# Moving row squares between VectorE and ScalarE in an RMS-norm and GELU kernel

## Chip, cores, metric

The kernel runs on one core of one Trainium2 chip. The metric is the device time of an execution in microseconds (us); medians of several executions are given. The span of a profiled execution is about 2 us shorter than the time on the metric.

## The reference

```python
x: (8, 1024, 2048) float32, gamma: (2048,), eps = 1e-5
rms = np.sqrt(np.mean(x ** 2, axis=-1, keepdims=True) + eps)
out = gamma * x / rms
return 0.5 * out * (1 + np.tanh(np.sqrt(2 / np.pi) * (out + 0.044715 * out ** 3)))
```

67.1 MB come in and 67.1 MB go out, in float32.

## The kernel before

The 8192 rows are cut into 16 groups of 128 partitions by 4 rows (4096 KB each). Six groups fit in SBUF at a time, in six slots. For each group SyncE issues the load. ScalarE and VectorE square the four rows and sum each (ScalarE with an activation and accumulator, VectorE with a product of the row with itself). VectorE and GpSimd make 1/rms. VectorE multiplies the group by gamma, in place. ScalarE applies GELU with 1/rms as its scale, in place, and issues the store. A slot's next load waits until its store has landed. Groups 2 and 3 come in with one double load, and groups 12 and 13 go out with one double store. "Landing" is the moment at which the program learns that a transfer is complete.

```python
def on_vector(g):
    return 1 if g % 3 else 2        # how many of the 4 squares VectorE does

def squares(g, r, n):               # on ScalarE
    for q in range(r, r + n):
        nc.scalar.activation(out=junk, in_=slot[g % SLOTS][:, q, :],
                             func=ACT.Square, accum_out=ssq[:, g, q : q + 1])

def squares_on_vector(g, r, n):
    for q in range(r, r + n):
        row = slot[g % SLOTS][:, q, :].rearrange("p (a b) -> p a b", b=GW)
        nc.vector.scalar_tensor_tensor(out=spare[:, :, 0:GW], in0=row, scalar=1.0, in1=row,
            op0=ALU.bypass, op1=ALU.mult, accum_out=ssq[:, g, q : q + 1])

# ... (inverse_rms, scale, gelu, store as described above)

for g in range(G + 1):              # each engine runs its own share of this in this order
    if g < G:
        squares(g, 0, R - on_vector(g))
        squares_on_vector(g, R - on_vector(g), on_vector(g))
        # ... inverse_rms(g); scale(g, 0, R)
    if g:
        gelu(g - 1)
        store(g - 1)
        if g - 1 + SLOTS < G:
            load(g - 1 + SLOTS)
```

Note the order on ScalarE: the squares of group g stand ahead of the GELUs of group g - 1, and so ahead of the store of group g - 1.

Of the kernel before, what the change touches and what calls it, by code (L numbers as in the profile page):

```python
# [13 lines left out]
SLOTS = 6  # L14
# [10 lines left out]
def kernel(  # L25
# [51 lines left out]

    def on_vector(g):

        return 1 if g % 3 else 2  # L80

    def load(g):
        nc.sync.dma_start(out=slot[g % SLOTS], in_=part(x2, g))  # L83
# [70 lines left out]
    with tc.manual_schedule():  # L154
# [23 lines left out]
        for g in range(G + 1):  # L178
# [3 lines that stand above are left out]
                if g < G - 1:  # L182
                    inverse_rms(g)
                    scale(g, 0, R)
                else:
                    scale(g, 0, 1)
                    inverse_rms(g)
                    for r in range(1, R):
                        scale(g, r, 1)
# [5 lines that stand above are left out]
# [35 lines left out]
```

## Time and profile before

| | before |
|---|---|
| time, median | 317.19 us (6 runs, 316.85 to 317.45) |
| span of the profiled run | 315.1 us |
| VectorE busy | 198.5 us, 63% |
| ScalarE busy | 206.9 us, 66% |
| load queue and store queue | 49.7% and 49.3% of 16 DMA engines |
| squares on ScalarE / VectorE | 42 / 22 |

The busy shares of the compute engines are averages over stages.

### The profile page before, as it was taken

How to read it: one execution, taken by the hardware profiler on the slowest of the kernel's cores; microseconds unless marked ns; L12 is line 12 of the kernel's file. 1: busy time of each engine (PE TensorE's matmuls, PEld its weight loads, DVE VectorE, ACT ScalarE, POOL GpSimd, SP SyncE). 2: the span in 40 equal slices, each digit the busy share in tenths (PEclk: the TensorE clock that was granted, in tenths of full speed). 3: DMA queues.
4: the chain of work that ended last, by engine and by line, in shares of the span. 5: the costliest groups of instructions: out<-in, count | busy, mean ns of one | idle time of the engine just before them, and what ended most of it. 6: DMA issues, size and time to landing. Idle time of an engine off the chain costs nothing.

```text
span 315.1 us, 457 instructions
## 1 busy us (share of the span) xinstructions
PE 7.2 (2%) x8; PEld 2.5 (1%) x8; DVE 198.5 (63%) x129; ACT 206.9 (66%) x150; POOL 16.4 (5%) x21
## 2 busy tenths in 40 slices
PE   0900000000000000000000000000000000000000
PEld 0300000000000000000000000000000000000000
DVE  0089887988989884639684393668727638781000
ACT  1327869999999749397590965929369295797000
POOL 0010101011010101010010100101001010010000
DMA  8999989999999999999999999999999999999896
GB/s 334 404 462 408 526 339 396 458 402 462 403 463 403 459 408 458 412 453 424 441 424 441 424 441 424 441 428 437 437 428 437 428 437 428 474 399 474 387 445 291
DMA packets 4498, 134.24 MB, mean 426 GB/s; under 512 B 512, under 2 KB 656, under 8 KB 656
## 3 DMA queue, kind: packets, MB, share of 16 engines
q1 hardware_dynamic: 2160, 67.11, 49.7%
q10 hardware_dynamic: 2336, 67.12, 49.3%
q14 instruction: 2, 0.02, 0.0%
HBM read 67.12 MB, written 67.11 MB: 426 GB/s over the span
## 4 chain that ended last, share of the span: by engine, by line
another core or an unknown queue 36%; DMA 36%; ACT 18%; issue 1%; SPq 1%; ACTq 0%
DMA pair<-in_x_dram 21%; DMA out_dram<-pair 15%; ACT pair L133 12%; ACT junk L87 6%; SPq L83 1%; ACTq L143 0%
## 5 line engine op out<-in xcount | busy, mean ns | idle before, releaser
L124 DVE TENSOR_TENSOR pair<-pair,gamma_ps 128x8192 f32<-128x8192 f32 (+1 forms) x19 | 139.2, 7334 | 0.0
L87 ACT ACTIVATE junk<-pair 128x2048 f32<-128x2048 f32 x42 | 79.0, 1881 | 78.7 <-DMA pair<-in_x_dram 76.2
L133 ACT ACTIVATE pair<-pair,rstd 128x2048 f32<-128x2048 f32 x64 | 122.6, 1987 | 2.3 <-DVE pair L124 1.9
L97 DVE SCALAR_TENSOR_TENSOR spare<-pair 128x2048 f32<-128x2048 f32 x22 | 50.4, 2291 | 39.3 <-DMA pair<-in_x_dram 24.6
L110 POOL TENSOR_TENSOR y<-ms,power 128x4 f32<-128x4 f32 x16 | 16.1, 1007 | 260.8 <-DVE ms L105 260.8
L105 DVE TENSOR_SCALAR ms<-ssq 128x4 f32<-128x4 f32 x16 | 2.7, 170 | 26.2 <-ACT junk L87 25.4
L113 DVE TENSOR_TENSOR z<-ms,y 128x4 f32<-128x4 f32 x16 | 2.6, 163 | 19.0 <-POOL y L110 19.0
L87 ACT ACTIVATION_READ_ACCUMULATOR junk<-pair 128x1 f32 x42 | 7.8, 186 | 0.0
L171 PE MATMUL gamma_ps<-spare,ones 1*128 1x512 f32 x8 | 7.2, 1072 | 8.3 <-DMA spare<-in_gamma_dram 8.3
L117 DVE SCALAR_TENSOR_TENSOR rstd<-z,y 128x4 f32<-128x4 f32 x16 | 2.6, 162 | 0.6
L114 DVE SCALAR_TENSOR_TENSOR z<-z,y 128x4 f32<-128x4 f32 x16 | 2.6, 162 | 0.6
L171 PEld LDWEIGHTS gamma_ps<-spare,ones 1*128 1x128 f32 x8 | 2.5, 326 | 11.4 <-issue 11.4
L169 ACT ACT_TABLE_LOAD x1 | 1.3, 1283 | 1.4 <-PEq L211 1.4
L97 DVE DVE_READ_ACCUMULATOR spare<-pair 128x1 f32 x22 | 1.8, 83 | 0.0
L167 DVE MEMSET warm<- 1x1 f32 x1 | 0.1, 59 | 0.8 <-PEq L211 0.8
L169 ACT ACTIVATE warm<-warm 1x1 f32<-1x1 f32 x1 | 0.2, 202 | 0.0
L168 DVE MEMSET ones<- 1x128 f32 x1 | 0.2, 165 | 0.0
L166 POOL MEMSET power<- 128x4 f32 x1 | 0.1, 101 | 0.3 <-POOLq L211 0.3
L211 POOL MEMSET const-float32-0.0<- 128x1 f32 x1 | 0.1, 98 | 0.2 <-issue 0.2
L211 POOL MEMSET const-bfloat16-1.0<- 128x1 bf16 x1 | 0.1, 102 | 0.0
L211 POOL MEMSET const-uint8-127<- 128x1 uint8 x1 | 0.1, 102 | 0.0
L211 POOL MEMSET const-float32-1.0<- 128x1 f32 x1 | 0.1, 98 | 0.0
## 6 DMA issues: line engine op xcount, KB each, us to landing
pair<-in_x_dram SPq DMA_DIRECT2D x14, 4096.0 KB, 25.5
out_dram<-pair ACTq DMA_DIRECT2D x13, 4096.0 KB, 52.4
out_dram<-pair ACTq DMA_DIRECT2D x1, 4032.0 KB, 31.3
out_dram<-pair ACTq DMA_DIRECT2D x1, 64.0 KB, 17.6
spare<-in_gamma_dram ACTq DMA_DIRECT2D x1, 8.0 KB, 7.4
pair<-in_x_dram SPq DMA_DIRECT2D x1, 40.5
out_dram<-pair ACTq DMA_DIRECT2D x1, 30.9
```

Of the source, the lines that this page charges most:

```text
L83: nc.sync.dma_start(out=slot[g % SLOTS], in_=part(x2, g))
L87: nc.scalar.activation(out=junk, in_=slot[g % SLOTS][:, q, :], func=ACT.Square, accum_out=ssq[:, g, q : q + 1],)
L97: nc.vector.scalar_tensor_tensor(out=spare[:, :, 0:GW], in0=row, scalar=1.0, in1=row, op0=ALU.bypass, op1=ALU.mult, accum_out=ssq[:, g, q ...
L105: v.tensor_scalar(out=ms, in0=ssq[:, g, :], scalar1=1.0 / D, scalar2=eps_f, op0=ALU.mult, op1=ALU.add,)
L110: nc.gpsimd.tensor_tensor(out=y_, in0=m_, in1=power, op=ALU.pow)
L113: v.tensor_tensor(out=z_, in0=m_, in1=y_, op=ALU.mult)
L114: v.scalar_tensor_tensor(out=z_, in0=z_, scalar=-0.5, in1=y_, op0=ALU.mult, op1=ALU.mult)
L117: v.scalar_tensor_tensor(out=rstd[:, g, :], in0=z_, scalar=1.5, in1=y_, op0=ALU.add, op1=ALU.mult,)
L124: nc.vector.tensor_tensor(out=rows, in0=rows, in1=gamma_ps.unsqueeze(1).to_broadcast([P, n, D]), op=ALU.mult,)
L133: nc.scalar.activation(out=slot[g % SLOTS][:, r, :], in_=slot[g % SLOTS][:, r, :], func=ACT.Gelu_apprx_tanh, scale=rstd[:, g, r : r + 1],)
L169: nc.scalar.activation(out=warm, in_=warm, func=ACT.Gelu_apprx_tanh)
L171: nc.tensor.matmul(out=gamma_ps[:, k : k + 512], lhsT=ones, rhs=gamma_row[:, k // GW : (k + 512) // GW, 0:GW], start=True, stop=True,)
```

## The change

The intent is to relieve ScalarE while the slots fill for the first time, when it is busy nearly all the time, and to give VectorE less to do later on.

```diff
     def on_vector(g):
 
-        return 1 if g % 3 else 2
+        return 2 if g < SLOTS else 1
```

SLOTS is 6. The counts do not change: 22 squares on VectorE and 42 on ScalarE in both kernels.

## The prediction

> **What bounds the kernel now.** I read the page first: the strip of DMA load over the span, then the shares of the two queues. VectorE is busy for 63% of the span, ScalarE for 66%; neither is near full. The transfers are.
>
> ```profile
> DMA  8999989999999999999999999999999999999896
> DMA packets 4498, 134.24 MB, mean 426 GB/s; under 512 B 512, under 2 KB 656, under 8 KB 656
> q1 hardware_dynamic: 2160, 67.11, 49.7%
> q10 hardware_dynamic: 2336, 67.12, 49.3%
> ```
>
> q1 carries the loads of x, q10 the stores of the result. Together their packets fill 49.7 + 49.3 = 99.0% of the time of 16 engines: of 315.1 us only about 3 us are not transfer. To see where those 3 us lie, I asked for the busy table in six stretches that follow the kernel's stages: start, loads alone, the mixed stage while the slots fill and drain for the first time, the steady state, stores alone, end.
>
> ```profile
> 0.00:5.00 5.00, 0.00 (x0) 0.00 (x0) 0.22 (x2) 1.49 (x2) 0.31 (x5) 1.00 0.68 236
> 5.00:45.00 40.00, 7.16 (x8) 2.49 (x8) 26.77 (x17) 20.50 (x17) 2.02 (x2) 1.00 1.00 432
> 45.00:110.00 65.00, 0.00 (x0) 0.00 (x0) 55.75 (x39) 61.09 (x44) 5.03 (x5) 1.00 1.01 432
> 110.00:270.00 160.00, 0.00 (x0) 0.00 (x0) 102.14 (x62) 104.96 (x77) 8.05 (x8) 1.00 1.00 433
> 270.00:310.00 40.00, 0.00 (x0) 0.00 (x0) 13.61 (x12) 18.90 (x12) 1.01 (x1) 1.00 1.00 433
> 310.00:315.00 5.00, 0.00 (x0) 0.00 (x0) 0.00 (x0) 0.00 (x0) 0.00 (x0) 1.00 0.52 223
> ```
>
> The last two columns are DMA share and GB/s; before them stand length, then busy us of PE, weight load, VectorE, ScalarE and GpSimd, and the clock. From 5 to 310 us the engines are full at 432 to 433 GB/s, whether they load, store or do both. The only gaps are the first 2 us before any packet moves and the run-out after the last. So 134.24 MB / 0.4325 = 310.4 us, plus about 2 us of start, 0.7 us of run-out and 1 to 2 us around them, is the 315.1 us span. A change that moves no bytes has nothing to win here; it can only lose, by leaving a queue empty.
>
> Note the stretch 45 to 110: ScalarE is busy 61.09 of 65 us there, and VectorE 55.75. This is the stage that the change is aimed at, and the one that looks compute-bound if the DMA column is overlooked.
>
> The second question is how far the stores are issued ahead of need. The page's list of DMA issues, with KB each and median us from issue to landing:
>
> ```profile
> pair<-in_x_dram SPq DMA_DIRECT2D x14, 4096.0 KB, 25.5
> out_dram<-pair ACTq DMA_DIRECT2D x13, 4096.0 KB, 52.4
> ```
>
> A group is 4096 KB = 4.19 MB; alone it needs 4.19 / 0.432 = 9.7 us, and with both queues alternating 19.4 us. A store takes 52.4 us, so the typical one stands in its queue for about 52.4 - 19.4 = 33 us before a byte of it moves. The chain of waits shows the same for one store:
>
> ```profile
> 81.91 45.95 DMA out_dram<-pair
> ```
>
> Store 3 was issued at 81.91 and landed at 127.86.
>
> **What the Trainium skill says.** "Perfetto Trace Analysis", section "Roofline", says that one core alone is bounded by its 16 DMA engines at about 435 GB/s in total; the 432 to 433 GB/s above agree, and say that there is no headroom. "DMA: Bandwidth & Descriptors", section "Queues, rings and completion order", says that each DMA engine takes turns between the queue rows for which it has work. The trace agrees: from 45 to 110 us q1 moved 14.61 MB and q10 13.42 MB. A queue with anything in it therefore gets its half, and the engines idle only if both are empty. "ScalarE: Activation LUTs", section "What ACT_TABLE_LOAD costs", gives an activation with immediate operands as 186 ns + 0.833 ns per element, 1892 ns for 2048; the Square activations here took 1881 ns, so the price of a moved square is the ordinary one.
>
> **The change part by part.** Counts first. Before, groups 0, 3, 6, 9, 12 and 15 have two squares on VectorE: 16 + 6 = 22. After, groups 0 to 5 have two: 12 + 10 = 22. ScalarE keeps 42. Nothing is added or removed: groups 1, 2, 4, 5 hand one square each to VectorE, groups 6, 9, 12, 15 take one each back. Busy times stay near 198.5 and 206.9 us.
>
> Steps as the timeline has them, start to start. On VectorE: a group with one square takes 12.83 us (73.84 to 86.67), with two 15.15 us (58.69 to 73.84); the 8.68 us scaling of the group is the last part. On ScalarE: a square 2.03 us, four Gelus 7.66, store issue to next square 0.4.
>
> Early stage. VectorE starts group 1 at 30.64 as before. With 15.15 us each, groups 2 to 6 start at 45.8, 60.9, 76.1, 91.2, 106.4 (before: 43.5, 58.7, 73.8, 86.7, 99.5), and each group's scaling ends as the next starts. ScalarE now has only 2 squares and finishes them early, then waits for the scaling:
> - store 1: squares of group 2 from 42.16, done 46.2; Gelus to 53.9 (before 55.83, so 1.9 us earlier);
> - store 2: scaling done 61.0, plus 7.7: 68.7 (before 67.86);
> - store 3: 76.2 + 7.7 = 83.9 (before 81.91);
> - store 4: 91.3 + 7.7 = 99.0 (before 95.97);
> - store 5: 106.5 + 7.7 = 114.2 (before 108.00, so 6.2 us later).
>
> So the change moves the early bound from ScalarE to VectorE and makes stores 2 to 5 later by 0.8, 2.0, 3.0 and 6.2 us. What does this cost? Store 0 is untouched and lands at 69.8, where load 6 is issued. From there a store lands every 19.4 us, so store 1 has its turn at about 69.8, store 2 at 89, store 3 at 108.5 (landing 127.86, as measured), store 4 at 128, store 5 at 147. Issued at 53.9, 68.7, 83.9, 99.0 and 114.2 they are 16, 20, 25, 29 and 33 us early. Cost: 0.
>
> Group 6 has one square: VectorE starts group 7 at 106.4 + 12.8 = 119.2. Its load landed at 114.79; ScalarE does its three squares from then to 120.9, and store 6 goes out at 128.5, just as before. From there loads set the rhythm again and the delay is forgotten.
>
> Steady state. In groups 9 and 12 ScalarE does three squares, so stores 8 and 11 go out 2.03 us later (165.15 to 167.2, 223.22 to 225.2). ScalarE then waits 7.74 us for the next load in those periods and would wait 5.7 us, as in its other groups. Cost: 0.
>
> Tail. This is the only place where a later store could show at the end.
>
> ```profile
> 269.65 1.88 ACT L87 ACTIVATE junk<-pair 128x2048 f32<-128x2048 f32 x1 [5.67 <-DMA pair<-in_x_dram]
> ...
> 281.29 0.34 ACTq L143 DMA_DIRECT2D out_dram<-pair  x1
> 281.67 7.68 ACT L133 ACTIVATE pair<-pair,rstd 128x2048 f32<-128x2048 f32 x4 [0.42 <-ACT pair L133]
> 289.38 0.34 ACTq L143 DMA_DIRECT2D out_dram<-pair  x1
> ```
>
> The last load lands at 269.65; group 15 now has three squares on ScalarE, so store 14 goes out at 281.29 + 2.03 = 283.3 and store 15 at 291.4. VectorE keeps up: its inverse waits for the third square at 275.7, and the last scaled row is ready at about 284.3, well before the last Gelu asks for it near 289.5. The double store of groups 12 and 13 was issued at 264.01 and took 30.9 us (its own line of the issue list), so it lands at 294.9. Store 14 moves from then, store 15 from 294.9 + 9.7 = 304.6. Both are still 11.6 and 13.2 us early. Cost: 0.
>
> Sum: 0.0 us. I predict 317.2 us, the time before.
>
> **The rivals.** First, VectorE becomes the bound in the early stage. It does: from 15 to 119 us it is nearly always busy. If this stage were on the path, the late store 5 would add up to 6.2 us, for 323.4 us (2.0% slower). Against it: the 20 us and more by which these stores lead the queue, and that q10 isn't empty.
>
> Second, the intent works: if the 61.09 of 65 us of ScalarE were the bound of the early stage, four squares taken off would give 4 x 2.03 = 8.1 us, 309 us (2.6% faster). Against it: the 1.01 DMA share of the same stretch, and that 310.4 us of bytes alone forbid it.
>
> Third, the tail shows its 2.03 us in full: 319.2 us. It would if the queue ran dry before 291.4; for that over 11 us of backlog would have to be gone.
>
> Fourth, the other mix of early loads and stores changes the DMA rate itself. The rate is 432 or 433 in all stages, so I would give this 0.5 us at most, either way.
>
> **Range and chances.** The three runs before spread over 0.6 us. The central case is exactly 0, each margin is over 10 us, and what is left is noise and the third rival in part: 316.6 to 318.0 us. Faster by over 2% (below 310.9) is ruled out by the bytes: 0.01. Slower by over 2% (above 323.6) needs an error in the backlog: 0.02. Within 2%: 0.97.
>
> **What would show each step.** Right: q1 and q10 again 49 to 50% each and DMA share 1.00 in the stretches between 5 and 310 us; load 6 issued near 69.8 us; store 5 issued near 114, stores 14 and 15 near 283.3 and 291.4; median landing of the stores shorter by their later issue, with the same landing times; ScalarE waiting for the scaling between 60 and 107 us. Wrong: a stretch after 45 us with a DMA share below 0.97, loads from the seventh on issued later than before, or an end of the span after 316 us.

## More of the kernel before

The waits say who sits idle for whom. Two lines of the waits of the kernel before (who waited, for whom, us in total, times, longest us):

```profile
ACT junk L87 <- DMA pair<-in_x_dram: 76.2, 12, 10.1
ACT pair L133 <- DVE pair L124: 1.9, 1, 1.9
```

L87 is the Square on ScalarE, L133 the GELU, L124 the scaling by gamma on VectorE. ScalarE waits for loads for 76 us in all, and for VectorE's scaling only once.

## The result and the profile after

| | before | after |
|---|---|---|
| time, median | 317.19 us (6 runs, 316.85 to 317.45) | 317.22 us (6 runs, 316.98 to 317.27) |
| span of the profiled run | 315.1 us | 315.3 us |
| VectorE busy | 198.5 us | 198.5 us |
| ScalarE busy | 206.9 us | 207.4 us |

The ratio is 1.0, with a 95% interval of 0.9987 to 1.0013. Ratios here are the mean time of one kernel's fast runs over that of the other's fast runs of the same rounds, so they are not quite the ratio of the medians quoted.

The page of the changed kernel, load strip and queues:

```profile
DMA  8999989999999999999999999999999999999896
q1 hardware_dynamic: 2160, 67.11, 49.8%
q10 hardware_dynamic: 2336, 67.12, 49.3%
```

The strip is the same digit for digit. The busy table of the changed kernel in the six stretches of the prediction (last two columns: DMA share and GB/s; of the numbers with a count (x), the third and fourth are VectorE and ScalarE busy us):

```profile
0.00:5.00 5.00, 0.00 (x0) 0.00 (x0) 0.22 (x2) 1.49 (x2) 0.31 (x5) 1.00 0.71 242
5.00:45.00 40.00, 7.16 (x8) 2.49 (x8) 26.61 (x18) 18.46 (x15) 2.02 (x2) 1.00 1.00 432
45.00:110.00 65.00, 0.00 (x0) 0.00 (x0) 58.44 (x40) 53.20 (x38) 4.76 (x5) 1.00 1.01 430
110.00:270.00 160.00, 0.00 (x0) 0.00 (x0) 101.61 (x61) 113.11 (x84) 8.34 (x9) 1.00 1.00 433
270.00:310.00 40.00, 0.00 (x0) 0.00 (x0) 11.60 (x10) 21.11 (x14) 1.01 (x1) 1.00 1.00 433
310.00:315.00 5.00, 0.00 (x0) 0.00 (x0) 0.00 (x0) 0.00 (x0) 0.00 (x0) 1.00 0.58 249
```

The DMA columns of this view count a packet (mostly 32 KB, 1.2 us here) whole in the stretch in which it begins: a short stretch can read above 1.00, and 0.00 means that no packet begins.

From 45 to 110 us ScalarE went from 61.09 to 53.20 us and VectorE from 55.75 to 58.44. The work moved, as intended; the DMA columns hardly did (share 1.01 in both, 432 and 430 GB/s). The waits of the changed kernel, the same two lines:

```profile
ACT junk L87 <- DMA pair<-in_x_dram: 66.0, 12, 10.3
ACT pair L133 <- DVE pair L124: 13.9, 5, 3.9
```

ScalarE now waits five times for VectorE's scaling, 13.9 us in all. It waits 10 us less for loads. This is one idle time in exchange for another. The timeline shows it at one place of the early stage, and the stores at the tail:

```profile
61.21 7.68 ACT L133 ACTIVATE pair<-pair,rstd 128x2048 f32<-128x2048 f32 x4 [2.94 <-DVE pair L124]
...
114.39 0.34 ACTq L143 DMA_DIRECT2D out_dram<-pair  x1
...
283.52 0.34 ACTq L143 DMA_DIRECT2D out_dram<-pair  x1
...
291.62 0.34 ACTq L143 DMA_DIRECT2D out_dram<-pair  x1
```

The GELUs of group 2 start 2.94 us after ScalarE is free, when the scaling is done. Store 5 is issued at 114.39, 6.4 us later than before, and stores 14 and 15 at 283.52 and 291.62, 2.2 us later. The median time of a store from issue to landing fell accordingly:

```profile
out_dram<-pair ACTq DMA_DIRECT2D x13, 4096.0 KB, 50.4
```

It was 52.4. Stores that are issued later stand in the queue for less, and land when they landed before: every store of the changed kernel landed within 0.5 us of its landing before (store 3 at 128.20 in place of 127.86).

### The profile page after: what moved, and what is told of

Its sections match the earlier page's. It is cut to its first block, busy times and chain, and to the rows that moved or that the text cites. A ratio compares the mean times of both kernels' runs of the same rounds, so it can differ in the third digit from the quotient of the medians.

```text
span 315.3 us, 455 instructions
## 1 busy us (share of the span) xinstructions
PE 7.2 (2%) x8; PEld 2.5 (1%) x8; DVE 198.5 (63%) x129; ACT 207.4 (66%) x150; POOL 16.4 (5%) x21
## 3 DMA queue, kind: packets, MB, share of 16 engines
q1 hardware_dynamic: 2160, 67.11, 49.8%
q10 hardware_dynamic: 2336, 67.12, 49.3%
## 4 chain that ended last, share of the span: by engine, by line
DMA 42%; DVE 22%; ACT 17%; another core or an unknown queue 6%; PE 2%; issue 2%; POOL 2%; SPq 0%; ACTq 0%; DVEq 0%; POOLq 0%
DMA pair<-in_x_dram 24%; DMA out_dram<-pair 15%; DVE pair L124 14%; ACT pair L133 11%; DVE spare L97 7%; ACT junk L87 5%; DMA spare<-in_gamma_dram 2%; PE gamma_ps L171 2%; POOL y L110 2%; DVE ms L105 0%; DVE z L113 0%; DVE z L114 0%; DVE rstd L117 0%; SPq L83 0%
## 5 line engine op out<-in xcount | busy, mean ns | idle before, releaser
L133 ACT ACTIVATE pair<-pair,rstd 128x2048 f32<-128x2048 f32 x64 | 122.7, 1988 | 14.3 <-DVE pair L124 13.9
## 6 DMA issues: line engine op xcount, KB each, us to landing
pair<-in_x_dram SPq DMA_DIRECT2D x14, 4096.0 KB, 25.4
```

The costliest lines, as they stand in the source:

```text
L133: nc.scalar.activation(out=slot[g % SLOTS][:, r, :], in_=slot[g % SLOTS][:, r, :], func=ACT.Gelu_apprx_tanh, scale=rstd[:, g, r : r + 1],)
```

## The experiments

The median of the kernel before in the same rounds was 317.02, 316.97 or 317.0 us. The theory: the DMA engines are full, and each store is issued long before the store queue reaches it, so that moved squares cost or gain nothing. The rivals: the early and the late half of the change cancel; VectorE or the tail is on the path; moving squares between these engines costs nothing anywhere.

### The halves of the change alone

```diff
# early half alone
-        return 1 if g % 3 else 2
+        return 2 if g < SLOTS or g % 3 == 0 else 1
# late half alone
-        return 1 if g % 3 else 2
+        return 2 if g < SLOTS and g % 3 == 0 else 1
```

> The early half of the change alone: two squares on VectorE in groups 0 to 5, two in every third group after that, as before. Theory (full DMA engines, both halves cost nothing): 317.2 us, within 0.3. Rival (the halves cancel: the early half gains or loses by itself what the late half gives back): off 317.2 by 2 us or more, in the opposite sense to the late half. If the later store 5 (114.3 in place of 108.0) were on the path: 323. Stores 14 and 15 are issued near 281.5 and 289.6 as before the change.

Measured: 317.15 us (5 runs), ratio to before 1.0002 (0.999 to 1.0015).

> The late half alone: groups 0 to 5 as before, one square on VectorE in every group from 6 on. Theory: 317.2 us, within 0.3; stores 14 and 15 issued 2.0 us later, near 283.5 and 291.6, with the same end. Rival (the tail shows its square): 319.2. Rival (halves cancel): off by 2 us or more, opposite to the early half.

Measured: 317.24 us (5 runs), ratio 1.0007 (0.9995 to 1.002). Stores 14 and 15 were issued at 283.27 and 291.36.

Neither half moves the median by more than some 0.2 us (the wider interval leaves room for 0.6), so no gain and loss of 2 us or more cancel. Each is hidden by itself.

### How large the margins are: the tail

The changed kernel, with row 0 of group 15 squared n more times on ScalarE ahead of the last GELUs (n = 4, then 8; the result stays right):

```diff
                 squares(g, 0, R - on_vector(g))
+                if g == G - 1:
+                    for _ in range(n):
+                        squares(g, 0, 1)
```

> The changed kernel with row 0 of group 15 squared four more times on ScalarE (8.1 us, result unchanged) ahead of the last Gelus. Stores 14 and 15 go out near 291.6 and 299.7. By the margins (the store queue reaches them at 294.9 and 304.6 in the kernel before) both are still in time: 317.2 us, within 0.4. Rival (the tail is on the path): 325.3 us. If a store needs some 3 us or more between issue and first packet even at the head of the queue, up to 1 us shows.

Measured: 317.24 us (4 runs), ratio 1.0008 (0.999 to 1.0026). 8.1 us of extra work on ScalarE directly ahead of the last two stores cost nothing.

> The same with eight more squares (16.3 us). Store 14 goes out near 299.8, 5 us after the queue is empty at about 295; store 15 near 307.9, before store 14 has moved. Theory: 5 us of empty engines and about 2 us from issue to first packet, so 322 to 325 us, with a DMA share well below 1.00 between 295 and 302 us. Rival (tail on the path from the start): 333 us. Rival (the margin is larger than counted): 317.

Measured: 323.67 us (4 runs, 323.45 to 323.79), ratio 1.0207 (1.0192 to 1.0223). The busy table from 295 to 302 us, first with four extra squares:

```profile
295.00:302.00 7.00, 0.00 (x0) 0.00 (x0) 0.00 (x0) 4.66 (x3) 0.00 (x0) 1.00 1.01 435
```

and with eight, together with the two 3 us stretches after 293 us:

```profile
295.00:302.00 7.00, 0.00 (x0) 0.00 (x0) 6.18 (x6) 6.58 (x4) 0.72 (x1) 1.00 0.35 150
...
293.00:296.00 3.00, 0.00 (x0) 0.00 (x0) 1.78 (x4) 3.00 (x3) 1.01 (x1) 1.00 0.00 0
296.00:299.00 3.00, 0.00 (x0) 0.00 (x0) 2.96 (x4) 3.00 (x2) 0.00 (x0) 1.00 0.00 0
```

With four, the engines are full (1.01). With eight, store 14 goes out at 299.77, the queue has run dry, and from 293 to 300 us no packet begins. The packet records of this trace (start and duration of each) tell more exactly when nothing moves: the engines finish the double store between 293.8 and 294.8 us, close to the 295 expected, and the first packet of store 14 begins at 300.61, 0.84 us after its issue, where the expectation had about 2. The time lost against the changed kernel is 323.67 - 317.22 = 6.45 us, and the engine time that stands idle in these records between 290 and 303 us is 6.6 us for all 16 engines, so the dry queue accounts for the whole loss. Both kernels behave as the margins say, and the two together bracket the margin: 8.1 us are free and 16.3 us cost 6.45, so the margin is about 16.3 - 6.45 = 9.8 us on top of the 2.2 us that the change itself used. That is 12 us for store 14 of the kernel before, where the prediction had 11.6 + 2.0 = 13.6. The 0.84 us from issue to first packet, which the prediction left out, is a good half of the difference (the Trainium skill, "DMA: Bandwidth & Descriptors", section "Latency and other measured facts", gives about 0.6 us to the first byte, a little less than this trace shows); the ragged end of the double store, up to 1 us, can account for most of the rest.

### How large the margins are: the early stage

The changed kernel with three squares of each of the first six groups on VectorE, with four, and with four and the last row squared a second time:

```diff
-        return 2 if g < SLOTS else 1
+        return 3 if g < SLOTS else 1        # three;  4 for the runs with four
...
                 squares_on_vector(g, R - on_vector(g), on_vector(g))
+                if g < SLOTS:                       # only in the run "four and one again"
+                    squares_on_vector(g, R - 1, 1)
```

Three:

> Three of the four squares of groups 0 to 5 on VectorE, 17.5 us a group. Estimate: stores 1 to 5 issued near 58, 76, 93, 111 and 128, so 11 to 19 us ahead of their turns at 70, 89, 108.5, 128 and 147. Theory: 317.2 us within 0.4, and a spread as small as that of the kernel before. The load of group 5 waits here for gamma's transfer, as in the run with four squares (the build gives it a shared semaphore); if that wait is what made those runs scatter from 317.4 to 319.8, these scatter too.

Measured: 317.04 us (5 runs, 316.87 to 317.51), ratio 1.0001 (0.9989 to 1.0013). Stores 1 to 5 were issued at 58.39, 75.89, 93.38, 110.87 and 128.36, as estimated. Store 5 is 20 us later than in the kernel before, and the time is the same. The extra wait of one load did no harm.

Four, twice:

> All four squares of groups 0 to 5 on VectorE: 19.8 us for each of these groups. Estimate from the durations of the traces: store 0 issued at 43 (38.6 in the changed kernel), stores 1 to 5 at about 63, 83, 103, 122 and 142, against turns in the store queue at 70, 89, 108.5, 128 and 147. So each is still about 5 us ahead, and the theory says 317.2 us, within 0.6. Rival (VectorE sets the early stage, any delay shows): store 5 is 28 us later than in the changed kernel, so up to 345 us; a rival in which lateness costs in part as it grows: 319 or more.

Measured: 317.39, 317.79 and 319.80 us, and one run of 324.93; ratio 1.0041 (1.0011 to 1.0071).

> The run with all four early squares on VectorE again, with more rounds: its fast executions read 317.39, 317.79 and 319.80 us, one slower 324.93. If the 5 us of margin are about used up, the same scatter comes back (317 to 320, now and then more), and the run with three squares lacks it. If the scatter was that chip's, all five agree within 0.6 us of 317.5.

Measured: 318.35 to 320.5 us in five runs, and one run of 324.8 labelled slow; ratio 1.0084 (1.0064 to 1.0104). The label rests on the time alone (over 1.5% above the fastest; the granted clock is 1.0 as in the others), and no other kernel here has such a run, so these two may belong to the scatter; the ratios leave them out. The scatter came back on another occasion and the kernel with three squares lacks it, so it belongs to this kernel. My expectation that a margin of some 5 us is as good as a larger one was wrong by 0.4 to 0.8%.

The engines did not run out of work here before the end: in the profiled run of 320.0 us the DMA share was 1.00 or 1.01 in every stretch from 5 to 310 us. But the load queue did run empty once. The two queues from 72 to 76.5 us (packets, MB, share of 16 engines), first in this run, then in the changed kernel:

```profile
q10 hardware_dynamic: 67, 2.10, 110.7%
q1 hardware_dynamic: 15, 0.00, 0.2%
...
q10 hardware_dynamic: 33, 1.08, 55.6%
q1 hardware_dynamic: 46, 0.98, 50.7%
```

The expectation noted that store 0 would be issued later, but gave it no margin to overdraw. Its landing starts load 6, the first load that has to wait for a slot. In this run store 0 was issued at 43.17 in place of 38.59, landed at 72.89 in place of 70.06, and so load 6 went out 2.8 us later, when the first loads had all moved. The store queue filled the engines meanwhile, so none stood idle, but the loads stayed late: the last one landed at 273.87 in place of 269.83. In the other profiled run with four squares (317.79 us) the last load landed at 271.36. With three squares store 0 still landed at 69.47 and the last load at 268.49.

What differs in time is the run-out. The busy table of that run after 310 us:

```profile
310.00:312.00 2.00, 0.00 (x0) 0.00 (x0) 0.00 (x0) 0.00 (x0) 0.00 (x0) 1.00 0.95 410
312.00:314.00 2.00, 0.00 (x0) 0.00 (x0) 0.00 (x0) 0.00 (x0) 0.00 (x0) 1.00 0.46 197
314.00:316.00 2.00, 0.00 (x0) 0.00 (x0) 0.00 (x0) 0.00 (x0) 0.00 (x0) 1.00 0.19 82
```

and of the changed kernel:

```profile
310.00:312.00 2.00, 0.00 (x0) 0.00 (x0) 0.00 (x0) 0.00 (x0) 0.00 (x0) 1.00 1.06 459
312.00:314.00 2.00, 0.00 (x0) 0.00 (x0) 0.00 (x0) 0.00 (x0) 0.00 (x0) 1.00 0.38 164
```

After 310 us there are 2 x (410 + 197 + 82) = 1378 KB left against 2 x (459 + 164) = 1246, only 132 KB more, which is 0.3 us for all 16 engines. But from 314 to 316 us the share is 19%, as much as some three of the sixteen engines, and the last packet ends at 317.0 us in place of 314.2. So most of the 2.9 us by which this span is longer lies in engines that have come apart: a single store keeps all of them busy in the tail (1.06 from 310 to 312 us), and the time runs until the last of them has finished. The median load took 28.8 us to land in this run, 25.4 in the changed kernel. Why they come apart when stores are issued some 5 us ahead, and not at 11 us or more, no run here shows; that stays open. The empty load queue is a candidate. A run in which store 0 alone goes out late would test it; none was made.

Four and one again:

> As the run with four squares on VectorE, and the square of row 3 done a second time there in groups 0 to 5 (the result stays right): 22.2 us a group. Estimate: stores 1 to 5 issued at 68, 90, 112, 134 and 156, so store 2 misses its turn by 1 us, store 3 by 3.5, store 4 by 6 and store 5 by 9. Theory: now it costs, between 3 and 9 us in all (320 to 326 us), since the load queue covers a part of the gaps; the DMA share falls below 1.00 between 100 and 180 us. If it still costs nothing, the margins as I counted them are too small; if the four-square run already costs, they are too large.

Measured: 325.26 us (4 runs, 325.13 to 325.86), ratio 1.0258 (1.0243 to 1.0274). Stores 1 to 5 were issued at 67.4, 89.5, 111.6, 133.7 and 155.8. The busy table of this run:

```profile
45.00:110.00 65.00, 0.00 (x0) 0.00 (x0) 60.75 (x44) 21.78 (x13) 3.03 (x3) 1.00 1.00 422
110.00:150.00 40.00, 0.00 (x0) 0.00 (x0) 37.22 (x27) 17.20 (x13) 2.01 (x2) 1.00 0.95 382
150.00:270.00 120.00, 0.00 (x0) 0.00 (x0) 94.63 (x63) 110.67 (x83) 9.06 (x9) 1.00 0.99 421
```

Against the 430, 433 and 433 GB/s of the changed kernel, the three stretches fall short by 65 x 8/430 = 1.2 us, 40 x 51/433 = 4.7 us and 120 x 12/433 = 3.3 us of transfer. That is 9.2 us, against a span that is 323.7 - 315.3 = 8.4 us longer. The share column shows only 40 x 0.05 + 120 x 0.01 = 3.2 us of it, so a share near 1.00 alone does not prove that nothing is lost: the rate must be read too. Once stores miss their turns, the loss shows as missing bytes per second, and it is never made up, because the engines are full afterwards.

### Without the cover of the transfers

To see whether moving the squares costs anything by itself, the traffic was cut and the computation left as it was. Loads from group 6 on fetch half the columns, stores write half; the other columns are stale, so the result is wrong.

```diff
-        nc.sync.dma_start(out=slot[g % SLOTS], in_=part(x2, g))
+        c = D if g < SLOTS else D // 2
+        nc.sync.dma_start(out=slot[g % SLOTS][:, :, 0:c], in_=part(x2, g)[:, :, 0:c])
...
-                nc.scalar.dma_start(out=part(o2, g), in_=slot[g % SLOTS])
+                nc.scalar.dma_start(out=part(o2, g)[:, :, 0 : D // 2],
+                                    in_=slot[g % SLOTS][:, :, 0 : D // 2])
# the double store and store 0 are cut in the same way
```

The kernel before:

> The kernel before with traffic cut on purpose (wrong result, stale columns): loads from group 6 on fetch half the columns, stores write half. 79.7 MB in place of 134.2, so 184 us of transfer at 432 GB/s; compute untouched. If the transfers are what hides the change, this kernel is bound by VectorE and ScalarE: last store issued near 241 us and about 249 us in all. If something else than bytes bounds the kernel, it stays near 317.

Measured: 248.75 us (4 runs, 248.66 to 248.84); 46.15 MB read and 33.55 MB written. The busy table:

```profile
15.00:120.00 105.00, 0.41 (x1) 0.00 (x0) 91.15 (x62) 90.32 (x67) 8.06 (x8) 1.00 0.99 402
120.00:235.00 115.00, 0.00 (x0) 0.00 (x0) 104.13 (x66) 109.36 (x79) 8.05 (x8) 1.00 0.68 253
```

The DMA share falls to 0.68 in the second stretch; VectorE and ScalarE are both busy for over 90% of it. In the first stretch, where the first six loads still move in full, the share is 0.99, so there the cover is thinner rather than gone.

The changed kernel:

> The changed kernel with the same cut. Without the cover of the transfers the change should show: six groups at VectorE's 15.15 us, then ten at ScalarE's 14.06 us, last store issued near 250 us, about 258 us in all: 8 to 9 us (3.5%) slower than the kernel before with the same cut. Rival (moving squares costs nothing anywhere, the engines have room): the same as that kernel. Rival (the intent: relief of ScalarE early helps): faster than it.

Measured: 259.82 us (4 runs, 259.78 to 259.92), 11.07 us or 4.5% slower than the kernel before with the same cut, and more than the 8 to 9 us that were expected.

```profile
15.00:120.00 105.00, 0.56 (x1) 0.00 (x0) 94.67 (x62) 79.12 (x59) 7.05 (x7) 1.00 0.97 397
120.00:235.00 115.00, 0.00 (x0) 0.00 (x0) 95.51 (x59) 110.16 (x83) 8.05 (x8) 1.00 0.61 230
```

In the first stretch ScalarE is busy for 79.12 us in place of 90.32, and in the second VectorE for 95.51 in place of 104.13. Each stage now has one engine that is busy for at least 90% of it and one that is less so.

The halves alone under the same cut:

> The early half of the change alone under the cut traffic (wrong result on purpose, as before). The kernel before took 248.75 us there, the changed one 259.82. VectorE does 15.15 us per group in groups 1, 2, 4 and 5 in place of 12.83, and stays behind: estimate 7 us more than 248.75, so 255 to 258. Rival (relief of ScalarE helps early, and the whole loss of 11 us is the late half's): 248 or less.

Measured: 255.82 us (4 runs), 7.07 us slower than the kernel before with the cut.

> The late half alone under the cut traffic. ScalarE does 14.06 us in every group from 6 on, in place of 12.1 in four of ten: estimate 5 to 7 us more than 248.75, so 253.5 to 256. The two halves need not add up to the 11 us of both, since in the early half VectorE is behind and in the late half ScalarE. Rival (only one of the halves costs): 249.

Measured: 256.24 us (4 runs), 7.49 us slower, a little above my 253.5 to 256. Who bounds each is read from the chain of waits, shares of the span by engine. The early half alone:

```profile
DVE 80%; POOL 6%; DMA 3%; PE 3%; issue 3%; DVEq 1%; ACT 1%; POOLq 1%
```

and the late half alone:

```profile
ACT 71%; DMA 16%; issue 7%; ACTq 3%; SPq 0%
```

With the early half VectorE carries the chain, with the late half ScalarE. The pattern before is balanced: over three groups VectorE needs 12.83 + 12.83 + 15.15 = 40.8 us, and ScalarE 14.06 + 14.06 + 12.1 = 40.2 us (14.06 is one period of ScalarE with three squares, 68.24 to 82.30 in the trace of before; 12.1 with two). The change makes it 45.5 against 36.3 in the early stage and 38.5 against 42.2 later. So the rival that these engines have room for the squares anywhere has fallen, and so has the one that relief of ScalarE helps: without the full traffic the change costs 11 us, and with it no cost can be seen.

No version tried beats the two kernels: the fastest kernel with a right result took 317.04 us, within the noise of both.

## Why the prediction was right

- **The bound.** The time lies at 317.22, for 317.2 predicted. A forecast of "no change" is hit by any account in which nothing shows, so the agreement of the number alone says little; the times of issue below and the experiments bear out the mechanism. The queues again fill 49.8% and 49.3%, and the rate from 5 to 310 us is 430 to 433 GB/s. The cut of the traffic confirms the bound from the other side: with 79.7 MB in place of 134.2 the kernel before took 248.75 us.
- **The counts and the moved work.** Busy times stayed within 0.5 us of those of before, as predicted.
- **The early stage.** Stores 1 to 5 were predicted at 53.9, 68.7, 83.9, 99.0 and 114.2. They came at 53.84, 68.91, 84.07, 99.23 and 114.39. VectorE did become the bound of this stage for computation (the first rival's premise), and ScalarE waited for it.
- **The early margins.** Predicted 16 to 33 us; the run with three squares took up to 14 us more of these away for nothing, and the run with four and one again, which by the same count overdrew them by up to 9 us, paid 8 us. The size is right. Load 6 went out at 70.13 us, 0.33 us later than in the trace of before; that is no more than traces of kernels with the same time differ (69.55 with three squares), so it is not taken for the sign of being wrong that the prediction names. What the prediction did not foresee, and the change does not reach, is that some 5 us of margin no longer hide everything, and that store 0, untouched by the change, has a margin of its own.
- **The steady state.** The squares given back in groups 9 and 12 cost nothing; the late half alone read 317.24.
- **The tail.** Predicted at 283.3 and 291.4, issued at 283.52 and 291.62. The margin of store 14 after the change, predicted at 11.6 us, is about 10 us as the two tail runs show it: the prediction counted from issue to turn and left out the 0.84 us to the first packet.
- **The rivals.** The first (323.4 us), the second (309 us) and the third (319.2 us) are excluded by the result, and the runs of the halves exclude that two of them cancelled.

## What to carry to other kernels

Here the DMA share was 1.00 in every stage, and a compute engine that is busy 94% of a stage did not bound it. Comparing how far ahead of its turn each store is issued with how much the change delays it gave the answer before the run; the time from issue to first packet belongs in that sum. The last few microseconds of margin were not free: with some 5 us left, the share was still 1.00 and the time rose by 0.4 to 0.8%. An unchanged time says nothing about the balance of the engines: with much of the cover taken away, the same change that measured 0 costs 4.5%. The chain of waits is to be read with this in mind. In the changed kernel it gives VectorE 22% of the span, because it follows a store back to its issue although that store then stood in the queue for longer than VectorE had delayed it.

## What the Trainium skill lacked or had wrong

- "DMA: Bandwidth & Descriptors", section "Where 436 GB/s comes from", says that for transfers between HBM and SBUF the HBM side binds, at about 358 GB/s. Here one core, with no other in the program, held 432 to 433 GB/s from 5 to 310 us with loads alone, stores alone and both. The passage doesn't say that its figure is the share with both cores of a pair at work; the section "Roofline", which the prediction draws on, makes that distinction and fits.
- "Vector Engine (DVE) Microarchitecture Reference", section "Points that are easy to get wrong", says that this instruction form with two sources in SBUF that are not bf16 runs at half throughput. The square on VectorE reads an fp32 row as both sources (one row, read twice) and took 2291 ns for 2048 elements, while the scaling by gamma, an ordinary product with one source in PSUM, took 2281 ns for as many. No halving shows.
- No page gives the price of reading an accumulator out: 186 ns on ScalarE and 83 ns on VectorE, with 2.03 and 2.33 us from one square to the next.
- That the engines of one transfer finish independently is said in "DMA: Bandwidth & Descriptors", section "Why a DMA increments its semaphore by 16 and not by 1"; no page says how far apart they can run out under full load. In one profiled run as much work as three of them do was still going on from 314 to 316 us, and the median load landed after 28.8 us in place of 25.4.
